# Seventeen column pairs by seven products instead of sixteen, with sums made in place, in a fused decoder layer

## The chip, the cores and the metric

The kernel runs as one program on one core of a Trainium2 chip. The metric is the device time of one execution in microseconds (us). The kernel before takes 706.92 us, the median of three runs (706.69, 706.92 and 707.40).

## The reference, cut to what matters

The layer takes x (512 tokens by 1024 features, float32) and a conditioning vector c. It computes a token mixer (block-sparse attention beside a Mamba-2 head group), a LayerNorm, a gated feed-forward part with a causal convolution of three taps, and a second LayerNorm. The change concerns the first LayerNorm's output and the feed-forward part:

```
mod = (c_act @ ada_w[i] + ada_b[i])[:, None, :]
sh1, sc1, g1, sh2, sc2, g2 = jnp.split(mod, 6, axis=-1)
...
x = layer_norm(DEEPNORM_ALPHA * x + (1.0 + g1) * y, ln1_g[i], ln1_b[i])
h = x * (1.0 + sc2) + sh2
...
def conv_ffn(h, w_up, conv_w, conv_b, w_down):      # D_FF = 2816
    u = causal_dwconv(h @ w_up, conv_w, conv_b)     # w_up: 1024 x 5632
    g, val = jnp.split(u, 2, axis=-1)
    return (jax.nn.silu(g) * val) @ w_down
```

## The kernel before, in words

All products are float32 split in two: each operand has a rounded high part and a low part (the rest), and one product is three matmuls, high by high, high by low and low by high (`mm3`). A weight tile is loaded to a buffer `raw`, ScalarE copies the high part out of it, and VectorE subtracts to get the low part.

**The order of all instructions** is written by a planner, the class `Order`. Each piece of work is a Python generator (a thread) with a priority; the planner has a price for each operation, plays the engines' clocks forward, and at each step emits, of the operations that could start soonest on an engine, the one of the best priority (a lower number is better). An `Alt` names two operations, on ScalarE or on VectorE, and the planner takes the one that would end sooner. Buffers come from classes with a fixed number of slots: class "s" (one 128 x 512 tile of float32) has 9, class "ps" (the banks of PSUM) has 8.

**LayerNorm 1.** `ln1` handles one of four token tiles t; `ln1_t` transposes half a tile (four 128 x 128 blocks) on TensorE into a bank `pt`, moves the four blocks out of PSUM to `hk` with a scale and a bias per partition, and splits `hk` into `h2h` (ScalarE) and `h2l` (VectorE). The move is an `Alt` (lines 1308 and 1309 of the kernel before). `quarters` then forms four sums of quarters of the input (`ts`).

**The up product.** `w_up` has 22 pairs of column tiles: pair j is gate tile j and value tile j, 128 columns each. An ordinary pair takes 2 tiles x 8 blocks x 3 = 48 matmuls with 512 moving columns. A pair in the list `SEVEN` (line 695) is one 2 x 2 block product done with seven half-size products instead of eight: 7 x 4 x 3 = 84 matmuls with 256 moving columns (`seven`), into four banks (`sP`). The pair's two raw tiles hold the quarters a11, a12 and, in the second tile, a21 and a22. `sums_seven` (line 716) makes s1 = a21 + a22 in place in the second raw tile and s3 = a21 + a11 in a buffer `sw`, each with a DMA that adds on landing, issued by GpSimd; SyncE loads a11 into that buffer first. `split_seven` (line 764) makes the two other sums on VectorE, s1 + a11 and that plus a12, in the order of the seven products (0, 1, 2, 4, 5, 6, 3), and splits each factor into a `wq` tile: `hi` is ScalarE's copy, `lo` VectorE's subtraction. At most ten weight tiles stand ready.

The priority of the splits is 0 when no more than one column tile (three and a half products) is ready ahead of TensorE, 3.5 up to two tiles, and 7 beyond. `seven_out` adds the seven results up on VectorE (seven adds of 256 columns), and `up_post` does the convolution (one ScalarE pass, two VectorE passes per tile), SiLU and the product of gate and value; both have priority 2. A bank is free again when its last reader has run. `keep`, with priority 2.5, later splits the products for the down projection; `dn` (the down projection) starts on four banks.

Of the kernel before, what the change touches and what calls it, by code (L numbers as in the profile page):

```python
# [11 lines left out]
AF = mybir.ActivationFunctionType  # L12
OP = mybir.AluOpType
# [3 lines left out]
P = 128  # L17
# [396 lines left out]
def layer_kernel(  # L414
# [21 lines left out]
    R = Order(nc)  # L436
    T, V, A, G, S, GD = (Engine(R, k) for k in ("PE", "V", "A", "G", "S", "GD"))
# [23 lines left out]
    def bank(group, name="ps", after=()):  # L461
        return Alloc("ps", [P, 512], F32, name, group, after)

    def buf(cls, shape, name, group=None, dt=F32):
        return Alloc(cls, shape, dt, name, group)
# [226 lines left out]
            rows_item(w_out, k, n)  # L692
    UP0 = len(items)
    NSPLIT = 4
    SEVEN = [3, 5, 6, 7, 8, 10, 11, 12, 13, 15, 16, 17, 18, 19, 20, 21]
    for j, i in up_tiles:
        cols_item(w_up, i * D_FF + j * P)
    for n in range(2):
# [4 lines left out]
    def w_load():  # L703
        yield Need("loads")
        for i, (shape, src) in enumerate(items):
# [4 lines left out]
            j = (i - UP0) // 2  # L710
            if i == UP0 + 2 * j + 1 and j in SEVEN:
                R.spawn(sums_seven(j, raw, items[i - 1][1][:, :4], src[:, :4]), 4)
# [3 lines left out]
    def sums_seven(j, r1, a11, a21):  # L716

        q = yield buf("s", [P, 4, P], "sw")
        yield S.dma_start(q, a11)
        yield GD.dma_start(r1[:, :4], r1[:, 4:], accum_op=OP.add)  # L720
        yield GD.dma_start(q, a21, accum_op=OP.add)
        QS[j] = q
        R.mark(("qs", j))

    def w_split():
        yield Need(("hk", KC - 1))
        for i, (shape, _) in enumerate(items):
            yield Need(("raw", i))
            raw = RAW.pop(i)
            if i >= len(items) - NFF // 2:  # L730
                yield Need("g2p")
                g2 = RES["rw"][:, 0, None, HS[1]].to_broadcast([P, 2, 512])
                yield V.tensor_mul(raw, raw, g2)
            if 0 <= i - len(items) + LATE_DN < 2:
                yield Need("fin")
                m = 2 * (i - len(items) + LATE_DN)
                hi, lo = RES["w"][:, m], RES["w"][:, m + 1]
            elif UP0 <= i < UP0 + 2 * NFF and (i - UP0) // 2 in SEVEN:
                if (i - UP0) % 2 == 0:
                    yield Need(("raw", i + 1))  # L740
                    yield from split_seven((i - UP0) // 2, raw, RAW[i + 1])
                R.free(raw)
                wpos[1] = i + 1
                continue
            else:
                own = i >= UP0 + NSPLIT
                hi = yield buf("b", shape, "wh", "w2" if own else "wh", F32R)
                lo = yield buf("b", shape, "wl", "w2" if own else "wl", F32R)
            yield A.activation(hi, raw, AF.Copy)
            yield V.tensor_sub(lo, raw, hi.bitcast(F32))  # L750
            R.free(raw)
            W[i] = (hi, lo)
            wpos[1] = i + 1
            lead[1] += 1
            R.mark(("w", i))
# [8 lines left out]
    def split_seven(j, r0, r1):  # L764

        yield Need(("qs", j))
        a11, a12, s1, a22, s3 = r0[:, :4], r0[:, 4:], r1[:, :4], r1[:, 4:], QS.pop(j)
        dst, src, tmp = {}, {0: a11, 1: s1, 4: s3, 5: a12, 6: a22}, {}

        def make(m, x, y):  # L770
            t = tmp[m] = yield buf("s", [P, 4, P], "sw")
            yield V.tensor_add(t, x, y)
            src[m] = t

        def hi(m):
            dst[m] = yield buf("b", [P, 2, 4, P], "wq", "w2", F32R)
            yield A.activation(dst[m][:, 0], src[m], AF.Copy)

        def lo(m):
            q = [dst[m][:, 1], src[m], dst[m][:, 0].bitcast(F32)]  # L780
            yield V.tensor_sub(*q)
            WS[j, m] = dst[m]
            lead[1] += 2 / 7
            R.mark(("ws", j, m))

        yield from hi(0)
        yield from hi(1)
        yield from make(2, s1, a11)
        yield from lo(0)
        yield from lo(1)  # L790
        yield from hi(2)
        yield from lo(2)
        yield from hi(4)
        yield from make(3, src[2], a12)
        R.free(tmp[2])
        yield from lo(4)
        R.free(s3)
        for m in (5, 6, 3):
            yield from hi(m)
            yield from lo(m)  # L800
        R.free(tmp[3])

    def w_next():
        i = wpos[0]
        wpos[0] += 1
        if not (UP0 <= i < UP0 + 2 * NFF and (i - UP0) // 2 in SEVEN):
            lead[0] += 1
# [447 lines left out]
    def xn_done(t):  # L1255
        uses[t // 2] -= 1
        if not uses[t // 2]:
            R.free(XN[t // 2])
# [9 lines left out]
    def ln1(t, ps):  # L1268
        yield Need(("po", t, 0), ("xr", t), "g1p")
        st = yield buf("t", [P, 2, 6], "st")  # L1270
        mv = yield buf("t", [P, 4], "mv")
        r, g1p = XR[t], ROWS["g1p"]
        for n in range(2):
            yield Need(("po", t, n))
            y = yield buf("s", [P, 512], "yp")
            yield V.tensor_mul(y, ps[t, n], g1p[:, HS[n]])
            R.free(ps[t, n])
            yield V.scalar_tensor_tensor(r[:, HS[n]], r[:, HS[n]], ALPHA, y, op0=OP.mult, op1=OP.add)
            R.free(y)
            yield V.bn_stats(st[:, n], r[:, HS[n]])  # L1280
        yield from ln_stats(st, mv)
        yield V.scalar_tensor_tensor(mv[:, 3:4], mv[:, 0:1], -1.0, mv[:, 2:3], op0=OP.mult, op1=OP.mult)
        if t % 2 == 0:
            XN[t // 2] = yield buf("e", [P, 2, DM], "XN")
            R.mark(("XN", t // 2))
        yield Need(("XN", t // 2), "mcol", "h2")
        xn = XN[t // 2][:, t % 2]
        for n in range(2):
            yield Alt(A.activation(xn[:, HS[n]], r[:, HS[n]], AF.Identity, bias=mv[:, 3:4], scale=mv[:, 2:3]),
                      V.tensor_scalar(xn[:, HS[n]], r[:, HS[n]], mv[:, 2:3], mv[:, 3:4], op0=OP.mult, op1=OP.add))  # L1290
        R.free(r, st, mv)
        yield S.dma_start(xn_d[t], xn)
        xn_done(t)
        HK[t] = yield buf("b", [P, KC, P], "hk")
        for n in range(2):
            R.spawn(ln1_t(t, n), 1)

    def ln1_t(t, n):
        xn = XN[t // 2][:, t % 2]
        pt = yield bank("mix", "pt2")  # L1300
        yield [T.transpose(pt[:, i * P:(i + 1) * P], xn[:, (4 * n + i) * P:(4 * n + i + 1) * P], ident)
               for i in range(4)]
        xn_done(t)
        hk = HK[t][:, 4 * n:4 * n + 4]
        for i in range(4):
            k = 4 * n + i
            src, sc, bi = pt[:, i * P:(i + 1) * P], mcol[:, 0, k:k + 1], mcol[:, 1, k:k + 1]
            yield Alt(A.activation(hk[:, i], src, AF.Identity, bias=bi, scale=sc),
                      V.tensor_scalar(hk[:, i], src, sc, bi, op0=OP.mult, op1=OP.add))
        R.free(pt)  # L1310
        d = (slice(None), slice(4 * n, 4 * n + 4), slice(t * P, (t + 1) * P))
        h2h, h2l = H2["hl"]
        yield A.activation(h2h[d], hk, AF.Copy)
        yield V.tensor_sub(h2l[d], hk, h2h[d].bitcast(F32))
        R.mark(("h2", t, n))
# [402 lines left out]
    def ffn():  # L1718
# [22 lines left out]
        for n, (j, i) in enumerate(up_tiles[NSPLIT:]):  # L1741
            if j in SEVEN:
                if i == 0:
# [115 lines left out]
```

## Time and profile before

| | |
|---|---|
| median of 3 runs | 706.92 us (706.69 to 707.40) |
| the profiled execution: its own time, and its span | 707.04 us, 705.3 us |
| TensorE matmuls busy | 690.0 us (98%) in 4197 |
| TensorE weight loads busy | 596.6 us (85%) |
| VectorE (DVE) busy | 623.6 us (88%) |
| ScalarE (ACT) busy | 362.7 us (51%) |
| GpSimd (POOL) busy | 99.5 us (14%) |
| chain that ended last, by engine | PE 83%, DVE 9%, DMA 3% |

Matmuls are pipelined and their ends are modelled: the start of one to the start of the next is what one costs. The same holds on VectorE and ScalarE, where a row's duration is about 0.08 us longer than the step from one start to the next. All helper calls stand under line 309, so groups are told apart by the names of the tiles (`out<-in`). The span falls into the mixer (to about 330 us), LayerNorm 1 with the first up tiles (to 386), the up product (to 575) and the down product with LayerNorm 2 (to the end).

### The profile page before, as it was taken

How to read it: one execution, taken by the hardware profiler on the slowest of the kernel's cores; microseconds unless marked ns; L12 is line 12 of the kernel's file. 1: busy time of each engine (PE TensorE's matmuls, PEld its weight loads, DVE VectorE, ACT ScalarE, POOL GpSimd, SP SyncE). 2: the span in 40 equal slices, each digit the busy share in tenths (PEclk: the TensorE clock that was granted, in tenths of full speed). 3: DMA queues.
4: the chain of work that ended last, by engine and by line, in shares of the span. 5: the costliest groups of instructions: out<-in, count | busy, mean ns of one | idle time of the engine just before them, and what ended most of it. 6: DMA issues, size and time to landing. Idle time of an engine off the chain costs nothing.

```text
span 705.3 us, 11343 instructions
## 1 busy us (share of the span) xinstructions
PE 690.0 (98%) x4197; PEld 596.6 (85%) x4197; DVE 623.6 (88%) x1182; ACT 362.7 (51%) x670; POOL 99.5 (14%) x103
## 2 busy tenths in 40 slices
PE   8999999999999999999999999999999999999995
PEld 7777877888888888887897899899899998888885
DVE  5888989899999999889999999999999999567646
ACT  2437568846677454224766556556556677211300
POOL 0011021101000000000102111111112100960023
PEclk9999999999999999999999999999999999999998
DMA  8997064143454727776576666766878474532202
GB/s 269 307 275 237 25 213 147 36 106 107 122 181 167 233 75 253 252 267 213 164 176 136 124 164 163 150 149 166 167 177 175 129 235 160 173 99 81 90 30 91
DMA packets 131323, 114.26 MB, mean 162 GB/s; under 512 B 4421, under 2 KB 110273, under 8 KB 131267
## 3 DMA queue, kind: packets, MB, share of 16 engines
q1 hardware_dynamic: 120515, 105.14, 48.3%
q0 software_dynamic: 10752, 8.39, 8.3%
q8 instruction: 33, 0.54, 0.3%
q14 instruction: 23, 0.19, 0.1%
HBM read 105.09 MB, written 4.23 MB: 155 GB/s over the span
## 4 chain that ended last, share of the span: by engine, by line
PE 83%; DVE 9%; DMA 3%; SPq 2%; issue 1%; ACT 1%; POOL 0%; DVEq 0%; POOLq 0%; ACTq 0%
PE sP L309 22%; PE fm L309 17%; PE dn L309 17%; PE po L309 6%; PE up L309 5%; PE first L309 4%; SPq L309 2%; PE tm L309 2%; PE psS L309 2%; PE pov L309 1%; PE pT L309 1%; DVE u L309 1%; PE py L309 1%; DMA wr<-in_mix_in_w_dram 1%; DMA csb<-drcs 1%
## 5 line engine op out<-in xcount | busy, mean ns | idle before, releaser
L309 DVE TENSOR_TENSOR wl<-raw,wh 128x1024 fp32r<-128x1024 f32 x70 | 88.0, 1260 | 25.8 <-ACT wh L309 25.6
L309 ACT ACTIVATE wh<-raw 128x1024 fp32r<-128x1024 f32 x70 | 73.5, 1054 | 68.8 <-DVE raw L309 23.3
L309 PE MATMUL dn<-wh,mid 128*128 128x512 f32 (+1 forms) x356 | 102.8, 371 | 0.0
L309 PE MATMUL sP<-ts,wq 128*128 128x256 f32 x768 | 96.4, 281 | 0.5 <-ACT m L309 0.5
L309 PEld LDWEIGHTS sP<-ts,wq 128*128 128x128 f32 x768 | 93.2, 188 | 0.8 <-ACT m L309 0.7
L309 PEld LDWEIGHTS dn<-wh,mid 128*128 128x128 f32 x356 | 64.5, 188 | 12.7
L309 PE MATMUL sP<-h2h,wq 128*128 128x256 f32 x384 | 74.2, 281 | 0.0
L309 PE MATMUL fm<-hh,wh 128*128 128x512 f32 x176 | 72.5, 412 | 0.0
L309 PE MATMUL fm<-hh,wl 128*128 128x512 f32 x176 | 69.3, 394 | 0.0
L309 PE MATMUL fm<-hl,wh 128*128 128x512 f32 x176 | 69.3, 394 | 0.0
L309 PE MATMUL dn<-wl,mid 128*128 128x512 f32 (+1 forms) x178 | 66.0, 371 | 0.0
L309 PEld LDWEIGHTS sP<-h2h,wq 128*128 128x128 f32 x384 | 61.5, 189 | 0.2
L309 PE MATMUL sP<-h2l,wq 128*128 128x256 f32 x192 | 53.9, 281 | 0.0
L309 PE MATMUL up<-h2h,wh 128*128 128x256 f32 (+1 forms) x128 | 43.2, 338 | 0.0
L309 PE MATMUL up<-h2l,wh 128*128 128x256 f32 (+1 forms) x128 | 43.2, 337 | 0.0
L309 PE MATMUL up<-h2h,wl 128*128 128x256 f32 (+1 forms) x128 | 43.2, 337 | 0.0
L309 DVE TENSOR_TENSOR wq<-raw,wq 128x512 fp32r<-128x512 f32 x64 | 42.9, 684 | 0.1
L309 PE MATMUL po<-wh,os 128*128 128x512 f32 x128 | 42.1, 396 | 0.0
L309 PEld LDWEIGHTS fm<-hh,wl 128*128 128x128 f32 x176 | 33.0, 188 | 7.7
L309 PEld LDWEIGHTS fm<-hh,wh 128*128 128x128 f32 x176 | 33.2, 188 | 7.1 <-issue 0.7
L309 ACT ACTIVATE wq<-raw 128x512 fp32r<-128x512 f32 x64 | 37.4, 622 | 3.1 <-PE sP L309 2.8
L309 PEld LDWEIGHTS dn<-wl,mid 128*128 128x128 f32 x178 | 33.4, 188 | 6.3
(269 smaller groups left out, 1542.9 us busy)
## 6 DMA issues: line engine op xcount, KB each, us to landing
raw<-in_ffn_up_w_dram SPq DMA_DIRECT2D x44, 512.0 KB, 4.1
raw<-in_mix_in_w_dram SPq DMA_DIRECT2D x26, 512.0 KB, 5.3
ad<-in_ada_w_dram SPq DMA_DIRECT2D x24, 512.0 KB, 4.1
raw<-in_ffn_down_w_dram SPq DMA_DIRECT2D x22, 512.0 KB, 4.0
aw<-in_ada_w_dram SPq DMA_DIRECT2D x32, 256.0 KB, 5.7
raw<-in_mix_out_w_dram SPq DMA_DIRECT2D x12, 512.0 KB, 3.8
csb<-drcs SPq DMA_DIRECT2D x8, 512.0 KB
ad<-in_ada_w_dram SPq DMA_DIRECT2D x4, 1024.0 KB
```

Of the source, the lines that this page charges most:

```text
L309: getattr(self.hw[op.eng], op.fn)(*op.args, **op.kw)
```

## The change

The list of pairs done by seven products has 17 entries instead of 16: pairs 4 and 9 are added, pair 8 is taken out. The two sums on VectorE are written over s1 in the raw tile instead of into two buffers of their own, and the first of them stands behind the splits of products 0 and 1 instead of before them. The blocks of the transposed input leave PSUM by ScalarE alone.

```diff
-    SEVEN = [3, 5, 6, 7, 8, 10, 11, 12, 13, 15, 16, 17, 18, 19, 20, 21]
+    SEVEN = [3, 4, 5, 6, 7, 9, 10, 11, 12, 13, 15, 16, 17, 18, 19, 20, 21]
...
-        dst, src, tmp = {}, {0: a11, 1: s1, 4: s3, 5: a12, 6: a22}, {}
-
-        def make(m, x, y):
-            t = tmp[m] = yield buf("s", [P, 4, P], "sw")
-            yield V.tensor_add(t, x, y)
-            src[m] = t
+        dst, src = {}, {0: a11, 1: s1, 2: s1, 3: s1, 4: s3, 5: a12, 6: a22}
...
         yield from hi(0)
         yield from hi(1)
-        yield from make(2, s1, a11)
         yield from lo(0)
         yield from lo(1)
+        yield V.tensor_add(s1, s1, a11)
         yield from hi(2)
         yield from lo(2)
         yield from hi(4)
-        yield from make(3, src[2], a12)
-        R.free(tmp[2])
+        yield V.tensor_add(s1, s1, a12)
         yield from lo(4)
         R.free(s3)
         for m in (5, 6, 3):
             yield from hi(m)
             yield from lo(m)
-        R.free(tmp[3])
...
-            yield Alt(A.activation(hk[:, i], src, AF.Identity, bias=bi, scale=sc),
-                      V.tensor_scalar(hk[:, i], src, sc, bi, op0=OP.mult, op1=OP.add))
+            yield A.activation(hk[:, i], src, AF.Identity, bias=bi, scale=sc)
```

## Rows read from the trace of the kernel before

**Rows 1.** The chain that ended last: start us, us, what.

```profile
392.35 11.15 PE up L309 x48
...
403.50 39.81 PE sP L309 x336
...
505.33 69.64 PE sP L309 x588
574.97 122.93 PE dn L309 x594
```

**Rows 2.** Busy time of the engines by stretch (windows).

```profile
370.00:386.40 16.40, 15.06 (x82) 12.47 (x81) 15.89 (x25) 10.72 (x20) 4.32 (x4) 1.00 0.56 136
...
505.00:575.00 70.00, 70.00 (x591) 69.91 (x590) 69.52 (x130) 43.72 (x79) 9.96 (x9) 1.00 0.72 173
```

**Rows 3.** Timeline of TensorE around the first seven-product pair, waits in brackets.

```profile
382.05 0.49 PE L309 MATMUL pad<-acch,ones_r 128*128 128x512 f32 x1
383.27 0.50 PE L309 MATMUL pad<-accl,ones_r 128*128 128x512 f32 x1 [0.73 <-DVE accl L309]
383.61 2.23 PE L309 MATMUL sP<-ts,wq 128*128 128x256 f32 x18
386.38 1.69 PE L309 MATMUL sP<-ts,wq 128*128 128x256 f32 x12 [0.54 <-ACT m L309]
```

**Rows 4.** Timeline of VectorE inside the last seven-product run.

```profile
559.58 0.68 DVE L309 TENSOR_TENSOR wq<-raw,wq 128x512 fp32r<-128x512 f32 x1
560.18 0.42 DVE L309 TENSOR_TENSOR u<-u,m 128x256 f32<-128x256 f32 x1
560.52 0.68 DVE L309 TENSOR_TENSOR wq<-raw,wq 128x512 fp32r<-128x512 f32 x1
...
562.86 0.74 DVE L309 SCALAR_TENSOR_TENSOR u<-sP,fprm,u 128x511 f32<-128x511 f32 x1
563.51 0.68 DVE L309 TENSOR_TENSOR sw<-sw,raw 128x512 f32<-128x512 f32 x1
```

**Rows 5.** The blocks that leave PSUM: instructions by tile hk, and two timelines.

```profile
L309 ACT ACTIVATE hk<-pt,mcol x22: 440/453/466, 330.8 to 352.7; 128x128 f32<-128x128 f32 x22
L309 DVE TENSOR_SCALAR hk<-pt,mcol x10: 401/406/409, 337.1 to 354.6; 128x128 f32<-128x128 f32 x10
...
337.15 1.37 DVE L309 TENSOR_SCALAR hk<-pt,mcol 128x128 f32<-128x128 f32 x4
...
345.17 1.49 ACT L309 ACTIVATE hk<-pt,mcol 128x128 f32<-128x128 f32 x4
```

**Rows 6.** Timelines of VectorE and TensorE where banks change hands last.

```profile
564.72 0.74 DVE L309 SCALAR_TENSOR_TENSOR u<-sP,fprm,u 128x510 f32<-128x510 f32 x1
...
573.49 1.22 DVE L309 TENSOR_TENSOR wl<-raw,wh 128x1024 fp32r<-128x1024 f32 x1
574.62 0.74 DVE L309 SCALAR_TENSOR_TENSOR u<-sP,fprm,u 128x510 f32<-128x510 f32 x1
...
566.28 1.00 PE L309 MATMUL sP<-ts,wq 128*128 128x256 f32 x7
...
575.98 0.63 PE L309 MATMUL dn<-wh,mid 128*128 128x512 f32 x2
```

**Rows 7.** The last split factor on VectorE, and its product on TensorE (timelines).

```profile
567.51 0.69 DVE L309 TENSOR_TENSOR wq<-sw,wq 128x512 fp32r<-128x512 f32 x1
...
573.37 0.28 PE L309 MATMUL sP<-h2h,wq 128*128 128x256 f32 x1
```

**Rows 8.** DMA issues from 340 to 520 us: KB each, median us to landing.

```profile
sw<-in_ffn_up_w_dram SPq DMA_DIRECT2D x13, 256.0 KB, 6.3
raw<-raw POOLq DMA_DIRECT2D x13, 256.0 KB, 4.3
sw<-in_ffn_up_w_dram POOLq DMA_DIRECT2D x12, 256.0 KB, 5.6
```

**Rows 9.** Group of ScalarE's copies of sums, 386.4 to 575 us: busy, mean ns, idle before.

```profile
L309 ACT ACTIVATE wq<-sw 128x512 fp32r<-128x512 f32 x45 | 27.1, 624 | 12.6 <-DVE sw L309 11.7 <-PE sP L309 1.0
```

## The prediction

> **What bounds the kernel now.** I read three views in this order: the chain that ended last, the busy time by stretch, and the timelines of TensorE and VectorE around the places where one could wait for the other.
>
> The chain shows TensorE alone from 386 us on: groups of matmuls follow each other without a gap, through the up product (to 574.97) and through 122.93 us of down product [rows 1]. So from there each microsecond less of matmul is one less of time, as long as nothing comes late. The windows say what could. In the last run of seven-product pairs, 505 to 575, VectorE is busy 69.52 of 70 us, ScalarE 43.72 [rows 2]. VectorE has no room left there, and TensorE has none either: two engines are full at once.
>
> Before 386 us TensorE waited twice for the slower side: its matmul of `pad` started 1.22 us after the one before it where a step is 11.15 / 48 = 0.23 [rows 1] (0.99 lost to VectorE), and at 386.38 it came about 0.64 late (18 matmuls of 39.81 / 336 = 0.118 after 383.61 end at 385.74) because ScalarE moved an `m` late [rows 3].
>
> How near is VectorE to stopping TensorE later? The split factors are not the near side: the last one is ready at 568.20 and its product starts at 573.37, a lead of 5.2 us [rows 7]. The banks are. In the last seven-product run each pair costs VectorE more than TensorE gives it, the splits go first by priority, and what waits is the convolutions that set banks free. At the last pair a convolution ends at 565.46 and the second of the pair's products, which by the count of eight banks can start only after such an end, starts at 566.28; at the down product the like convolution ends at 575.36 and the second tile starts at about 576.21 (the second of two matmuls at 575.98) [rows 6]. Both margins are 0.8 to 0.85 us. The kernel before just fits.
>
> **The change part by part.** I work against the profiled execution's own 707.04 us, of which 1.74 lie outside its span. It stands 0.12 above the median of 706.92, inside the three runs.
>
> *One more seven-product pair, on TensorE.* An ordinary pair takes 11.15 us for 48 matmuls, four seven-product pairs take 39.81 and seven take 69.64, so 9.95 each [rows 1]. TensorE saves 11.15 - 9.95 = 1.20 us.
>
> *The same pair on VectorE.* Steps from start to start: 0.60 for 512 columns (559.58 to 560.18), 0.34 for 256 (560.18 to 560.52), 0.65 for a convolution pass (562.86 to 563.51) [rows 4], and 1.13 for the low part of a whole raw tile (573.49 to 574.62) [rows 6]. A seven-product pair: 7 subtractions and 2 sums at 0.60, 7 adds at 0.34 to 0.46, 4 passes at 0.65, the product at 0.60, together 5.4 + 2.5 + 2.6 + 0.6 = 11.1 us. An ordinary pair: 2 x 1.13 + 2.6 + 0.6 = 5.5 us. VectorE gets 5.6 us more.
>
> *The blocks that leave PSUM.* 10 of 32 went over VectorE, four of them in 1.37 us less the 0.08 of the tail, 0.32 each: VectorE is rid of 3.2 us between 337 and 355. ScalarE takes them at 1.49 / 4 = 0.37, 3.7 us more [rows 5]. ScalarE was busy 10.72 of 16.40 us just after [rows 2], and beside those blocks it only has weight copies that can stand back, so I cost this at nothing. If that cover is gone, a half tile's split comes 4 x 0.37 = 1.5 us later and TensorE waits at most that, once.
>
> *Sums in place.* The number and size of the sums is the same: no VectorE work either way. What is added is a chain: the first sum now waits for both uses of s1 (product 1's copy and subtraction), the copy for product 2 waits for the sum, the second sum for product 2's copy and subtraction. Behind that sum on VectorE stand the next subtractions and older convolutions, behind the waiting copy on ScalarE the next copies and the `m` that leaves a bank; TensorE sees it only if the 5.2 us lead is used up. ScalarE already waits 11.7 us in all for sums, over 45 copies [rows 9]. I take 0; the bounds are below nothing 0 (no work goes) and above 17 times a copy of 0.62, some 10 us, if VectorE had nothing else in those moments. The nearest row speaks for 0: VectorE idles 0.48 us in 70 [rows 2]. Two buffers of class "s" less per pair: nobody is seen waiting for one on TensorE, 0.
>
> *Queues.* The extra pair adds one load by SyncE and two adding DMAs by GpSimd, each 256 KB, landing 4.3 to 6.3 us after issue [rows 8]; DMA engines are busy 72% of the last run [rows 2]. I take 0, the value nearest to those rows, up to 3 us if the first pairs' buffers come late.
>
> *Sum.* By 577 us VectorE has 5.6 - 3.2 = 2.4 us more work, and TensorE wants to be there 1.2 earlier: VectorE falls 3.6 us further behind. The margin of 0.8 us is worth less in VectorE's time, since convolutions get only what splits leave, (9.95 - 5.4) of 9.95: 0.4 us. That leaves 3.2 us for which TensorE would wait at the banks. Two things give way. While TensorE stands, the lead is more than one tile, the split's priority falls from 0 to 3.5, and one of the two low parts of whole tiles issued from 573.49 on [rows 6] can come after the convolutions: 1.1. And VectorE's idle 0.5 us between 370 and 386.4 [rows 2] is filled: 0.5. So TensorE waits 3.2 - 1.1 - 0.5 = 1.6 us near 566 to 578, and the time changes by -1.20 + 1.6 = +0.4: 707.4 against 707.04, or 707.3 against the median. If nothing gives way it is +2.0 (708.9); if both low parts do, -0.7 (706.2). What TensorE wins before 386 it loses at the banks again, so I don't count it here.
>
> **Rivals.**
>
> *A, TensorE stays the bound.* The planner writes the whole order anew, and convolutions come out early enough (the buffers set free let them start sooner). Then the 1.20 us stand, and of the two waits before 386 (0.99 and 0.64) some go, because VectorE is 3.2 us ahead at 357: between -1.2 and -2.8, with half of them -2.0, 704.9 against the median. For it: a wait at the banks is reckoned from two margins [rows 6]; the chain shows none so far [rows 1]. Against it: both engines are full there [rows 2], and the order has no VectorE work to put off but the low parts counted above. The Trainium skill (Perfetto Trace Analysis, Identifying the Most-Contended Engine) says to compare VectorE's occupancy with TensorE's busy share of weight loads and to work on the fuller one first. By it TensorE comes first here, 69.91 against 69.52 of 70 us, and the time would fall by the 1.20 us to 705.7. The trace agrees on which is fuller, by 0.4 us; it also shows how little the other has left.
>
> *B, the sums in place make VectorE wait.* Place: sum, copy, subtraction of products 2 and 3 of every pair, from 370 to 565. If the order has nothing older for VectorE in the gap, it idles. It decides from the point where the idle time passes about 0.1 us a pair (17 x 0.1 = 1.7, more than the work that can give way); at 0.15 us a pair, 2.5 us come on top of the +0.4: 709.8. For it: ScalarE's 11.7 us of waits for sums [rows 9]. Against it: VectorE's 0.48 us of idle in 70, with a queue of old convolutions.
>
> *C, the change does little of what it says:* 22 of 32 blocks already went over ScalarE, and the planner puts other VectorE work where the 3.2 us were, while the low parts give way fully. Then both sides cancel at 706.9.
>
> **How the numbers follow.** A run of three tells about 0.2% from no change, 1.4 us: faster is under 705.5, slower over 708.3. The forecast has 0.41, its own range 706.2 to 708.9, of which some 0.29 is within and 0.12 slower. A has 0.39: 0.31 faster (some wait before 386 goes too), 0.08 within. B has 0.16, all slower. C has 0.04, half faster, half within. Together 0.33 faster, 0.39 within, 0.28 slower. The range reaches from A with all waits gone and a little luck in the order (703.8) to B with the upper bound of the forecast, cut where about one in ten is left (710.4).
>
> **What would show it.** Right: seven-product pairs at 9.95 us on TensorE, and 17 of them; no `hk` on VectorE; between 560 and 580 a gap of 1 to 3 us on TensorE in front of an `sP` or the first `dn` group, ended by VectorE's `u`; VectorE over 99% busy from 386 on. Wrong: if the chain is TensorE alone up to the down product, A holds, and the step that failed is VectorE's debt at the banks; if VectorE's idle time between 386 and 575 has grown by microseconds in front of `wq` or the sums, B holds. A wait elsewhere, as at the first `up` tiles (a late `h2l` behind ScalarE) or in front of pair 4 for its DMA sums, would be a step that I priced at nothing.

## The result, and the profile after

The changed kernel takes 710.96 us, the median of four runs (709.78 to 711.72), against 706.81 us for the kernel before in the same session (706.34 to 707.40). The ratio is 1.0053, 95% interval 1.0038 to 1.0068: slower by 4.2 us, and above the range of the prediction. The profiled execution is the fastest of the four, 709.78 us with a span of 707.8, so the profile explains 2.7 us against the 707.04 of before; the other 1.4 us of the difference of medians are not in it. Medians and ratios here and below leave out three single executions, one each of experiments 2, 3 and 10, in which the chip was far slower (845.61, 3864.88 and 2252.52 us).

The chain that ended last, of after (start us, us, what; some of its longest pieces), against [rows 1]:

```profile
392.95 8.82 PE sP L309 x72
...
410.43 1.89 DVE wq L309 x3
...
482.22 1.89 DVE wq L309 x3
...
555.72 3.10 PE sP L309 x24
...
567.20 3.12 PE sP L309 x24
...
578.82 121.58 PE dn L309 x588
```

and its shares by engine on the page of after:

```profile
PE 59%; DVE 26%; SPq 4%; issue 4%; DMA 4%; ACT 2%; DVEq 0%; POOL 0%; POOLq 0%; ACTq 0%
```

Where one row of 588 matmuls stood without a break, there are now short pieces of TensorE between pieces of VectorE. PE's share of the chain fell from 83% to 59%, DVE's rose from 9% to 26%. The windows of after (us, then PE, PEld, DVE, ACT, POOL busy; the second is the stretch of [rows 2], the third the whole last run of seven pairs up to the down product):

```profile
370.00:386.40 16.40, 16.29 (x99) 14.09 (x98) 16.09 (x26) 8.42 (x16) 1.62 (x2) 1.00 0.45 102
505.00:575.00 70.00, 65.97 (x551) 65.08 (x550) 69.24 (x129) 40.17 (x76) 10.12 (x9) 1.00 0.67 161
502.50:577.20 74.70, 70.67 (x590) 69.75 (x589) 73.91 (x135) 44.58 (x82) 10.12 (x9) 1.00 0.69 164
```

In [rows 2] TensorE filled its 70.00 us. Now it is idle for 4.03 of them, and VectorE is about as full as before (69.24 us busy, 69.52 in [rows 2]). The last run takes 74.7 us where it took 69.64.

The first part of the change did what it says: all 32 blocks are on ScalarE (compare [rows 5]), and the wait in front of the second `pad` matmul, 0.99 us in [rows 1, 3], is 0.28 (375.48 to 375.99, less a step of 0.23). The wait for `m` at 386.38 in [rows 3] has gone too: from 370 to 386.4 us TensorE is idle for 0.11 us, where it was for 1.34.

```profile
L309 ACT ACTIVATE hk<-pt,mcol x32: 441/457/465, 330.3 to 354.4; 128x128 f32<-128x128 f32 x32
```
```profile
375.48 0.40 PE L309 MATMUL pad<-acch,ones_r 128*128 128x512 f32 x1
375.99 0.50 PE L309 MATMUL pad<-accl,ones_r 128*128 128x512 f32 x1
```

And then it is given back. TensorE of after where banks change hands (start us, us; in brackets the wait and who ended it):

```profile
543.99 0.28 PE L309 MATMUL sP<-h2h,wq 128*128 128x256 f32 x1
545.62 4.53 PE L309 MATMUL sP<-ts,wq 128*128 128x256 f32 x36 [1.35 <-DVE u L309]
...
554.14 0.28 PE L309 MATMUL sP<-h2h,wq 128*128 128x256 f32 x1
555.72 0.36 PE L309 MATMUL sP<-h2h,wq 128*128 128x256 f32 x1 [1.30 <-DVE u L309]
...
565.54 0.28 PE L309 MATMUL sP<-h2h,wq 128*128 128x256 f32 x1
567.20 0.36 PE L309 MATMUL sP<-h2h,wq 128*128 128x256 f32 x1 [1.38 <-DVE u L309]
...
578.35 0.97 PE L309 MATMUL dn<-wh,mid 128*128 128x512 f32 x2
```

From start to start the three are 1.63, 1.58 and 1.66 us where a step is 0.12: 1.5 us lost each time, 4.5 together. At the second tile of `dn` 0.24 more are lost (the second of the two matmuls at 578.35 starts at 578.82, a step of 0.47 where 0.23 is usual). Each of these waits ends when VectorE's last convolution pass on a bank is done. With smaller losses spread over the up product, TensorE loses 7.0 us from 386 us to that tile (each matmul's step less the usual one), where the kernel before loses 0.7. VectorE of after around the third:

```profile
563.73 0.74 DVE L309 SCALAR_TENSOR_TENSOR u<-sP,nfw,u 128x511 f32<-128x511 f32 x1
564.38 0.68 DVE L309 TENSOR_TENSOR wq<-raw,wq 128x512 fp32r<-128x512 f32 x1
565.10 0.69 DVE L309 TENSOR_TENSOR raw<-raw,raw 128x512 f32<-128x512 f32 x1
565.71 0.69 DVE L309 TENSOR_TENSOR wq<-sw,wq 128x512 fp32r<-128x512 f32 x1
566.31 0.74 DVE L309 SCALAR_TENSOR_TENSOR u<-sP,nfw,u 128x510 f32<-128x510 f32 x1
566.97 1.53 DVE L309 SCALAR_TENSOR_TENSOR u<-sP,fprm,u 128x511 f32<-128x511 f32 x2
568.42 1.28 DVE L309 TENSOR_TENSOR wq<-raw,wq 128x512 fp32r<-128x512 f32 x2
...
571.71 1.23 DVE L309 TENSOR_TENSOR wl<-raw,wh 128x1024 fp32r<-128x1024 f32 x1
...
574.66 1.53 DVE L309 SCALAR_TENSOR_TENSOR u<-sP,nfw,u 128x511 f32<-128x511 f32 x2
576.10 1.22 DVE L309 TENSOR_TENSOR wl<-raw,wh 128x1024 fp32r<-128x1024 f32 x1
577.23 1.53 DVE L309 SCALAR_TENSOR_TENSOR u<-sP,fprm,u 128x511 f32<-128x511 f32 x2
```

The pass that frees the third wait's bank starts at 566.31 and ends at 567.05; TensorE goes on at 567.20. Between the two passes on this bank stand a split, a sum and another split. There is also a new step: 564.38 to 565.10 is 0.72 us, where the split behind the sum takes 0.60 (565.71 to 566.31). The sum in place overwrites what the split right before it reads. This holds for all 17 places of that kind in the up product of after (median step 0.717); in the kernel before the six splits with a sum behind them, which goes to a buffer of its own, take 0.60.

From start to start I then summed VectorE's time by kind, from the first `mv<-st` of LayerNorm 1 (about 327 us in both) to the first add of the last pair:

| us | before | after | difference |
|---|---|---|---|
| `wq` low parts | 68.25 (112) | 73.95 (119) | +5.70 |
| sums | 19.26 (32) | 20.58 (34) | +1.32 |
| seven-product adds | 37.84 (105) | 40.37 (112) | +2.53 |
| `wl` low parts | 13.60 (12) | 11.35 (10) | -2.25 |
| `hk` blocks | 3.40 (10) | 0 | -3.40 |
| convolution, products, others | 105.41 | 105.33 | -0.08 |
| all | 247.77 | 251.60 | +3.8 |

Seven more low parts at 0.609 (68.25 / 112) are 4.26; with sums, adds and `wl` the seventeenth pair costs 5.86. The blocks give 3.40 back. The 17 longer steps come to 17 x 0.117 = 2.0.

The row "all" (below, the ledger) is the time that passes on VectorE between the two marks, pauses included. It grows whenever the run takes longer there, so a ledger that grows with the time proves nothing by itself; the work does. With each instruction at its usual step (the lower quartile of its kind in both traces) VectorE's work is 237.2 us before and 239.4 after, +2.3. Longer steps in front of sums add 2.2 (19 between the marks, two of them before 386 us). The rest is 0.7 us less, mainly because the two passes of a convolution follow each other directly less often, which makes a step longer too (last section).

### The profile page after: what moved, and what is told of

It is laid out like the page before. It is cut to its first block, busy times and chain, and to the rows that moved or that the text cites. A ratio compares the mean times of both kernels' runs of the same rounds, so it can differ in the third digit from the quotient of the medians.

```text
span 707.8 us, 11466 instructions
## 1 busy us (share of the span) xinstructions
PE 690.1 (98%) x4233; PEld 597.3 (84%) x4233; DVE 634.8 (90%) x1186; ACT 368.1 (52%) x687; POOL 102.2 (14%) x105
## 4 chain that ended last, share of the span: by engine, by line
PE 59%; DVE 26%; SPq 4%; issue 4%; DMA 4%; ACT 2%; DVEq 0%; POOL 0%; POOLq 0%; ACTq 0%
PE fm L309 17%; PE dn L309 17%; DVE wq L309 8%; DVE u L309 8%; PE po L309 6%; SPq L309 4%; PE up L309 3%; DVE sP L309 3%; PE sP L309 2%; PE tm L309 2%; DMA aw<-in_ada_w_dram 2%; DVE wl L309 2%; PE psS L309 2%; DVE raw L309 1%; PE pov L309 1%
## 5 line engine op out<-in xcount | busy, mean ns | idle before, releaser
L309 PE MATMUL sP<-ts,wq 128*128 128x256 f32 x816 | 103.0, 281 | 1.7 <-DVE u L309 1.4
L309 PEld LDWEIGHTS sP<-ts,wq 128*128 128x128 f32 x816 | 99.0, 189 | 2.6 <-DVE u L309 1.6
L309 PE MATMUL sP<-h2h,wq 128*128 128x256 f32 x408 | 78.7, 281 | 2.8 <-DVE u L309 2.7
L309 DVE TENSOR_TENSOR wq<-raw,wq 128x512 fp32r<-128x512 f32 x102 | 68.7, 685 | 0.5 <-ACT wq L309 0.4
L309 PEld LDWEIGHTS sP<-h2h,wq 128*128 128x128 f32 x408 | 65.3, 189 | 3.7 <-ACT wq L309 3.0
L309 ACT ACTIVATE wq<-raw 128x512 fp32r<-128x512 f32 x102 | 60.0, 623 | 13.4 <-DVE raw L309 12.0
L309 PE MATMUL sP<-h2l,wq 128*128 128x256 f32 x204 | 57.2, 280 | 0.0
L309 PEld LDWEIGHTS sP<-h2l,wq 128*128 128x128 f32 x204 | 38.5, 188 | 0.1
L309 POOL TENSOR_TENSOR XN<-XN,l 128x512 f32<-128x512 f32 x16 | 30.9, 1950 | 50.0 <-DMA XN<-drxn 49.4
L309 PEld LDWEIGHTS fm<-hl,wh 128*128 128x128 f32 x176 | 33.2, 189 | 5.9
```

Of the source, the lines that this page charges most:

```text
L309: getattr(self.hw[op.eng], op.fn)(*op.args, **op.kw)
```

## The experiments

The theory of all runs, T1: what decides is VectorE's total work from LayerNorm 1 to the last seven-product pair; what it is over, TensorE waits for at the banks. The expectations call it theory 1 as well. A table behind experiment 12 sets the work beside TensorE's losses. Times are medians beside runs of the kernel before on the same chip; the ratio has its 95% interval.

**1. The changed kernel with the old list of 16 pairs** (ScalarE alone and sums in place stay).

```diff
-    SEVEN = [3, 4, 5, 6, 7, 9, 10, 11, 12, 13, 15, 16, 17, 18, 19, 20, 21]
+    SEVEN = [3, 5, 6, 7, 8, 10, 11, 12, 13, 15, 16, 17, 18, 19, 20, 21]
```

> The changed kernel with the old list of 16 pairs: sums in place and blocks by ScalarE alone stay. Theory 1 (VectorE's debt: the extra pair is 5.6 us of VectorE work that comes due at the banks): VectorE has 3.4 us less for the blocks and about 1.4 more for the sums than the kernel before, so TensorE waits at no bank at the end of the up product and some of its two waits before 386 us go: 705.0 to 706.8. Theory 2 (the sums in place, not the pair, make VectorE late): as slow as the changed kernel, 709 to 711, with waits at the banks again.

705.07 us, ratio 0.9981 (0.9968 to 0.9994). The loss comes with the seventeenth pair; the two other parts together win 1.3 us by the ratio.

**2 and 3. The kernel before with the blocks on ScalarE alone**, twice.

```diff
-            yield Alt(A.activation(hk[:, i], src, AF.Identity, bias=bi, scale=sc),
-                      V.tensor_scalar(hk[:, i], src, sc, bi, op0=OP.mult, op1=OP.add))
+            yield A.activation(hk[:, i], src, AF.Identity, bias=bi, scale=sc)
```

> The kernel before with the blocks by ScalarE alone, nothing else. Theory 1: VectorE has 3.4 us less, TensorE is the bound from 386 on, only waits before 386 can go: 705.0 to 706.9. Rival (ScalarE alone delays the split of LayerNorm 1): waits of TensorE in front of the first up tiles, 707.5 to 709.

> The kernel before with the blocks of the transposed input on ScalarE alone, 16 pairs and sums in buffers of their own, once more, for its profile. T1: the 3.2 us that VectorE is rid of show as fewer TensorE waits before 386 us and a larger margin at the last banks; 704.5 to 705.5. Rival (the earlier time was luck of the chip): 706 to 707.

704.85 us, ratio 0.9978 (0.9969 to 0.9987), and 704.81 us, ratio 0.9968 (0.9957 to 0.9980). This one line beats both kernels, and with the sums in place added (experiment 1) nothing more is won. The end of its chain, in the second of the two:

```profile
492.17 11.19 PE up L309 x48
503.36 69.44 PE sP L309 x588
572.79 122.76 PE dn L309 x594
```

TensorE's last run is unbroken and begins 2 us earlier than in [rows 1]. Before 386 us it loses 1.7 us (from the first mark) where the kernel before loses 3.3; that is won, and here it is kept. VectorE's ledger (327.16 to 572.79) is 245.6, 2.1 less than before.

**4. The kernel before with the sums in place only** (16 pairs, blocks as before).

> The kernel before with the sums in place, nothing else (16 pairs, blocks on either engine). Theory 1: VectorE has about 1.4 us more (steps of 0.72 instead of 0.60 where a sum overwrites what the instruction before it read), the margin of 0.4 us of VectorE time is passed by 1.0: 707.5 to 708.5. Theory 2: 709 to 711, since the chain copy, subtraction, sum leaves VectorE idle.

706.26 us, ratio 1.0001 (0.9992 to 1.0010): a miss, no time lost. The 16 longer steps are there (median 0.717), but the ledger grows by only 0.3, from 247.77 to 248.11: fewer convolution passes follow each other directly, and the pauses shrink. At 16 pairs the price is covered.

**5. The changed kernel with the product of gate and value on GpSimd** for the later pairs.

```diff
-            yield V.tensor_mul(k, g, u)
+            yield G.tensor_mul(k, g, u)
```

> The changed kernel with the product of gate and value of pairs 6 and up on GpSimd instead of VectorE (same values). Theory 1: VectorE loses 13 steps of 0.60 before the down product, 7.8 us, more than its debt; TensorE has no wait at the banks and the time goes to 704 to 706.5, unless GpSimd slows VectorE as it does in the down product. Theory 2: the sums' chain stays, 709 to 711. Rival: GpSimd holds VectorE up by more than 4 us and its 1.9 us per product keeps buffers: 711 or more.

707.13 us, ratio 1.0009 (0.9998 to 1.0019), a half: no wait at the last banks is left, and 2.7 to 3.8 us of the loss are gone (against experiment 6 and the first result), but 704 to 706.5 is not reached. The group of GpSimd's products (386 to 575 us):

```profile
L309 POOL TENSOR_TENSOR keep<-u,u 128x512 f32<-128x512 f32 x13 | 18.9, 1456 | 63.1 <-ACT u L309 61.6 <-DVE u L309 1.5
```

While VectorE is rid of 13 x 0.60 = 7.8 us, its ledger falls by 5.1 only, to 246.51. Six instructions of VectorE, five low parts and a sum, take 0.94 to 1.80 us where 0.68 is usual, 4.7 us together, each beside one of GpSimd's products (last section). A low part of a whole tile that now falls behind the second mark (1.1 us) and shorter pauses account for the rest. New waits of 0.7 to 1.1 us for ScalarE's `m` and VectorE's adds stand in the middle of the up product.

**6. The changed kernel again.**

> The changed kernel once more, for a second profile and beside the others: 710 to 712, with three waits of about 1.5 us at the banks near 545, 556 and 567.

709.85 us, ratio 1.0048 (1.0035 to 1.0061), with the three waits in the same places (546.19, 556.28 and 567.77, 1.3 us each in the rows).

**7. The changed kernel with the choice between ScalarE and VectorE for the blocks put back.**

> The changed kernel with the blocks on either engine again (17 pairs, sums in place). Theory 1 (VectorE's debt sets the time): VectorE has 3.4 us more, all of which comes due at the banks: 713 to 715. Rival (only the last run counts, the early part is made up for before it): 710 to 712, the same as the changed kernel.

711.65 us, ratio 1.0075 (1.0063 to 1.0087). VectorE's work is 3.2 us more, the time 1.8 us against experiment 6 (same chip). TensorE loses 1.7 us more before 386 us and 0.5 more behind it. The sign is T1's; the size is under its 713 to 715 and inside the rival's 710 to 712, so this run does not decide.

**8. Seventeen pairs, with pair 18 ordinary instead of pair 14:** a run of nine pairs in the middle and of three at the end, instead of seven at the end.

> The changed kernel with its 17 pairs placed otherwise: pair 18 is ordinary instead of pair 14, so no run at the end is longer than three, but one in the middle has nine. Theory 1 in its form of a total (all of VectorE's work up to the down product has to be done by then): 709.5 to 711.5, with the waits at another place. Rival (the long last run empties the banks): 705 to 707, no wait at the banks.

710.96 us, ratio 1.0072 (1.0056 to 1.0087), no faster than the changed kernel (experiment 6, same chip: 1.0048); the waits are now at the end of the run of nine:

```profile
493.68 4.53 PE L309 MATMUL sP<-ts,wq 128*128 128x256 f32 x36 [1.56 <-DVE u L309]
...
503.76 0.36 PE L309 MATMUL sP<-h2h,wq 128*128 128x256 f32 x1 [1.30 <-DVE u L309]
...
515.24 0.36 PE L309 MATMUL sP<-h2h,wq 128*128 128x256 f32 x1 [1.34 <-DVE u L309]
...
526.75 0.36 PE L309 MATMUL sP<-h2h,wq 128*128 128x256 f32 x1 [1.31 <-DVE u L309]
```

The last three come 11.5 us apart, one for each pair: the 9.95 of the pair and 1.5 of waiting, which is near the 11.1 us that the prediction reckoned for a pair on VectorE. So it's not the last pairs' place that costs: here as in the changed kernel the debt is paid at the end of a long run of seven-product pairs.

**9. Experiment 1 with nine needless additions on VectorE** (128 x 512, result unread, 5.4 us; in the pairs up to 13).

```diff
+        if j <= 13:
+            pad = yield buf("s", [P, 4, P], "pad")
+            yield V.tensor_add(pad, a11, a12)
+            R.free(pad)
```

> The kernel with 16 pairs, sums in place and blocks by ScalarE alone (705.07 measured), with one more addition of 128 x 512 on VectorE in each of nine pairs, whose result nobody reads: 5.4 us of VectorE work, no work elsewhere. Theory 1: it costs what the extra pair costs, 709.5 to 711, with waits at the banks at the end of the up product. Rival (the extra pair's DMAs, its early place or its banks cost the time, not VectorE's work): 705 to 706.5.

708.17 us, ratio 1.0027 (1.0016 to 1.0039): +3.1 over experiment 1, between the two forecasts. Of the 5.4 us of added work the ledger shows 3.3; shorter steps and pauses took up the rest. TensorE loses 2.6 us more after 386, and waits for `u` appear in front of a product and of the down product, as at 17 pairs:

```profile
565.99 4.52 PE L309 MATMUL sP<-ts,wq 128*128 128x256 f32 x36 [0.88 <-DVE u L309]
...
576.36 0.50 PE L309 MATMUL dn<-wh,mid 128*128 128x512 f32 x1 [0.19 <-DVE u L309]
```

The extra pair, with as much work (5.5 us), costs more, 4.8 us (705.07 to 709.85). Its ledger is 1.2 us longer than here; why steps and pauses shrink less beside it is not shown.

**10 and 11. The changed kernel with 5.9 us less VectorE work**, twice: 17 pairs, sums in place, the same matmuls, without the third tap's pass for the value tiles of pairs 5 to 13 (this kernel leaves out a part of the layer and serves for timing alone).

```diff
         for s, fw in ((1, f1), (2, f0)):
+            if s == 2 and 27 <= ch <= 35:
+                continue
```

> The changed kernel, with the second VectorE pass of the convolution left out for the value tiles of pairs 5 to 13 (nine passes of 0.65 us, so 5.9 us less VectorE work; the third tap of those tiles is then missing from what is computed). TensorE's work is unchanged. T1 (VectorE's total up to the last pair is what TensorE waits for at the banks): the 4.8 us of waits at 545 to 579 go, and the time falls from some 710 to 704.5 to 706. Rival (the seventeenth pair or the new order itself holds TensorE, by the split priority or by sums that come late, whatever VectorE's total): the waits stay where they are and the time is 708.5 or more.

> The changed kernel without the second VectorE pass for the value tiles of pairs 5 to 13 (the third tap of those tiles is missing from what is computed), once more, for its profile. T1: 703.5 to 705, and between 540 and 580 us no wait of TensorE of more than 0.5 us that a convolution pass ends. Rival (the time fell because TensorE was faster elsewhere): waits of together 3 us or more still stand there.

703.84 us, ratio 0.9952 (0.9939 to 0.9965), and 703.66 us, ratio 0.9959 (0.9943 to 0.9975). The end of the chain in the second:

```profile
490.26 11.06 PE up L309 x48
501.32 69.59 PE sP L309 x588
570.91 122.71 PE dn L309 x594
```

With 5.9 us less work on VectorE the last run is whole again, no wait at a bank is left, and the time falls by some 6 us (709.85 to 703.66). The passes left out belong to pairs 5 to 13 and the waits stood in the last three pairs, so it is the total that counts. With this relief the seventeenth pair gains on TensorE about what was reckoned, 1.20 us: experiment 10 stands 1.0 us under the 16 pairs of experiment 3, on the same chip. Only VectorE could not pay for it.

**12. Seventeen pairs, the first sum in a buffer of its own, the second in place in it.**

```diff
+        src[2] = src[3] = t = yield buf("s", [P, 4, P], "sw")
+        yield V.tensor_add(t, s1, a11)
         yield from lo(0)
         yield from lo(1)
-        yield V.tensor_add(s1, s1, a11)
...
-        yield V.tensor_add(s1, s1, a12)
+        yield V.tensor_add(t, t, a12)
```

> The changed kernel, but the first sum of a pair is made into a buffer of its own before the first low part, and only the second sum is made in place, in that buffer: 17 pairs, s1 not overwritten. T1 with the price of the sums in place (some 1.4 us of VectorE time in all, from longer steps where a sum overwrites what the instruction before it read): half or more of that price goes, VectorE's ledger falls from 251.6 by 0.7 to 1.4 us and the time from some 710 to 708.5 to 709.5. Rival (the sums in place cost nothing at 17 pairs, or the additional buffer costs as much): 709.8 to 711.

711.52 us, ratio 1.0061 (1.0043 to 1.0078): a miss. Only three long steps are left between 386 and 575, but the order came out otherwise. VectorE waits 1.33 us, by the profile for a DMA (`drg<-acc`), two splits come late, and TensorE waits 2.81 for one of them:

```profile
564.70 1.29 DVE L309 TENSOR_TENSOR keep<-u,u 128x512 f32<-128x512 f32 x2 [1.33 <-DMA drg<-acc]
566.03 0.69 DVE L309 TENSOR_TENSOR sw<-raw,raw 128x512 f32<-128x512 f32 x1
566.63 1.29 DVE L309 TENSOR_TENSOR wq<-raw,wq 128x512 fp32r<-128x512 f32 x2
```
```profile
567.38 0.79 PE L309 MATMUL sP<-h2h,wq 128*128 128x256 f32 x2 [2.81 <-DVE wq L309]
```

Both sums in buffers of their own have no run at 17 pairs: with all nine slots of class "s" taken the planner comes to a stop, so with this list the sums in place are also what lets the seventeenth pair in. What the sums in place cost in time at 17 pairs stays open: their longer steps are measured, but no run took them away and left the rest as it was.

**Work and losses side by side**, worked out from the traces (us). Work: VectorE's instructions between the two marks at their usual steps. Losses: the steps of TensorE's matmuls less the usual ones, from the first mark to 386, and from there to the second tile of `dn`.

| kernel | pairs | VectorE's work | ledger | TensorE's loss to 386 | after 386 |
|---|---|---|---|---|---|
| experiment 3 | 16 | 234.0 | 245.6 | 1.7 | 0.5 |
| experiment 1 | 16 | 234.0 | 247.1 | 1.5 | 1.2 |
| before | 16 | 237.2 | 247.8 | 3.3 | 0.7 |
| experiment 4 | 16 | 237.2 | 248.1 | 3.1 | 0.5 |
| experiment 9 | 16 | 239.4 | 250.4 | 2.0 | 3.8 |
| experiment 5 | 17 | 230.5 | 246.5 | 1.3 | 4.9 |
| experiment 11 | 17 | 233.5 | 245.8 | 1.2 | 1.4 |
| changed kernel | 17 | 239.4 | 251.6 | 1.3 | 7.0 |
| experiment 8 | 17 | 239.4 | 252.1 | 1.1 | 8.3 |
| experiment 12 | 17 | 239.4 | 253.3 | 1.4 | 8.7 |
| experiment 7 | 17 | 242.6 | 253.8 | 3.1 | 7.5 |

Up to 237.2 us of work TensorE loses little after 386; from 239.4 on it loses 3.8 us or more. Experiment 5 stands out, for another reason: GpSimd stretches single instructions of VectorE.

## Why the prediction was wrong

**Right: the place and the mechanism.** VectorE's debt shows as TensorE waits that the convolutions' `u` ends, at banks, in the last run and at the second tile of `dn`. Experiments 8 to 11 and the table tie the waits to VectorE's total work: with less they go, with more they come, and with the pairs placed otherwise they move.

**Right: the two engines' first terms.** TensorE's -1.20 fits experiment 10's 1.0 us under experiment 3. On VectorE 5.9 was measured for the extra pair, where the forecast had 5.6, and 3.4 for the blocks, where it had 3.2. That "what TensorE wins before 386 it loses at the banks again" held too: 2.0 us were won there (losses of 1.3 instead of 3.3), and in the changed kernel nothing of it reached the end.

**Wrong: "Two things give way", 1.6 us. This is the step that failed.** It turned the +2.0 that the prediction had without it into +0.4, and neither thing happened. Two low parts of whole tiles still stand ahead of the last convolutions (571.71 and 576.10 in the rows of after), as two did before (569.11, and 573.49 in [rows 6]). Of the two that the prediction counted, only the first could have given way: the second, at 576.14, came behind the convolution of 574.62 already. The order is shown; why the priority did not fall isn't settled (the planner plays forward clocks of its own, in which TensorE may not have waited). And VectorE's idle time wasn't filled: from 370 to 386.4 it fell by 0.2 only (0.51 to 0.31), and over the whole stretch from 328 it grew from 2.40 to 2.99 us. The windows of before and of after:

```profile
328.00:386.40 58.40, 56.19 (x369) 50.06 (x367) 56.00 (x104) 40.04 (x72) 9.89 (x10) 1.00 0.61 166
```
```profile
328.00:386.40 58.40, 57.57 (x387) 51.90 (x386) 55.41 (x97) 43.62 (x82) 9.88 (x11) 1.00 0.69 176
```

Without the blocks VectorE had less to do there, and not enough other work came forward to fill the gap.

**Wrong as well: the sums in place at 0.** The argument looked for a pause of VectorE and was right that there is none: after 386 it waits once, 0.4 us. Rival B, in which it idles, is therefore not what happened. Time was added all the same, in the step: 19 x 0.117 = 2.2 us, 0.13 a pair. That rival B had priced 0.15 a pair is luck, since its mechanism was another. The ledger is 3.8 us longer where the forecast had 2.4, so 1.4 of it remain.

Put into the prediction's sum, without the things that give way, TensorE loses 3.2 + 1.4 = 4.6 us. This is a net figure, since the sum leaves out what is won before 386. Measured are 6.35 more after 386 (7.03 against 0.68: the 4.76 of the four waits shown, the rest in small ones) and 1.95 fewer before (1.34 against 3.29), net 4.4. With the -1.20 that is 710.2. The profiled execution took 709.78; it was 0.4 us earlier already at the first mark (327.08 against 327.51), up to which both kernels run the same instructions, so this part of the difference is not the change's. The median of 710.96 has no profile. That the price of the sums in place moves the time is a sum, not an experiment: at 16 pairs it was covered (experiment 4), at 17 it couldn't be isolated (experiment 12).

**Rival A** had TensorE stay the bound, at 704.9. Its gain before 386 came, its end did not; it is what experiments 2 and 3 show without the extra pair. The rule that the prediction quoted from the Trainium skill (Perfetto Trace Analysis, Identifying the Most-Contended Engine), to work on the fuller engine first, gave 705.7, and the kernel took 710.96. TensorE was the fuller by 0.4 us in 70, and unloading it at VectorE's expense lost 4 us: where two engines are this close, naming the fuller one does not price a change that loads the other.

## What to carry to other kernels

Where two engines are both full, price an exchange of work on the engine that receives it, over its whole ledger up to the place where the other waits for it, and count as cover only what a row shows to be idle; a planner's priorities giving way is a hope until a run shows it. A sum written over its operand removes a buffer and can add to the step of the instruction before it, so compare starts, not durations. An engine's time between two marks holds its pauses too, so test a theory on its work. Try the parts of a change singly: here one line alone gave 705 us, and the seventeenth pair took it back.

## What the runs showed of the hardware that was not expected

A VectorE instruction of 128 x 512 that overwrites what the instruction right before it reads starts 0.717 us after that one's start, where 0.601 is usual. Its own duration in the row (0.69) doesn't show it. Two convolution passes in a row over the same `u` do likewise: the two from 566.97 on take 1.45 us to the next start (568.42), where two apart take 0.65 each.

In experiment 5 the mean step of VectorE's low parts went from 0.621 to 0.652 us, but the mean hides what happened: 114 of the 119 kept their 0.68 us in the row, and five took 0.94 to 1.80. The two cases, each a product of GpSimd and VectorE beside it (timelines of experiment 5; start us, us):

```profile
525.70 1.68 POOL L309 TENSOR_TENSOR keep<-u,u 128x512 f32<-128x512 f32 x1 [6.36 <-ACT u L309]
526.13 1.79 DVE L309 TENSOR_TENSOR wq<-sw,wq 128x512 fp32r<-128x512 f32 x1
...
542.72 1.29 POOL L309 TENSOR_TENSOR keep<-u,u 128x512 f32<-128x512 f32 x1 [2.83 <-ACT u L309]
543.04 0.42 DVE L309 TENSOR_TENSOR u<-sP,u 128x256 f32<-128x256 f32 x1
543.38 0.74 DVE L309 SCALAR_TENSOR_TENSOR u<-sP,nfw,u 128x511 f32<-128x511 f32 x1
```

The six products beside which VectorE began an instruction with both inputs in SBUF took 1.59 to 1.73 us, and that instruction took 0.94 to 1.80. The other seven ran beside instructions that read a bank of PSUM (only at their edges, for up to 0.2 us, did some of them touch one with both inputs in SBUF); they took 1.28 to 1.34 us, and VectorE's instructions kept their time. The same stands in the down product of the changed kernel: there VectorE's subtractions of 128 x 512 take 0.69 us alone and 1.78 beside GpSimd.
